# Sums of weight blocks tied to the heads of the attention, and feed-forward operands in six steps instead of five

## The chip, the cores and the metric

The kernel runs on one core of one Trainium2 chip. The core has five engines that run side by side, each through an instruction list of its own, in order: TensorE (PE, matrix products), VectorE (DVE), ScalarE (ACT), GpSimd (POOL) and SyncE (SP), which issues transfers. POOL and ACT issue transfers as well. The metric is the time of one execution on the device in microseconds (us), less is better.

## The reference

The reference is one decoder block in float32 over a sequence of 1024 tokens of width 1024. Two branches read one normalised input, are merged by gates and pass one output projection. Then follow a cross-attention into 256 memory tokens, a feed-forward part and a last norm.

```python
u = rms_norm(h, norm_mix[l])
proj = u @ w_in[l]
u_ssm, q, k, v, f_logit, gate_logits = jnp.split(proj, [...], axis=-1)
y_ssm = jax.nn.gelu(s5_ssm(u_ssm, ...))              # 32 groups, 64 states each
glu_a, glu_b = jnp.split(y_ssm @ w_glu[l], 2, axis=-1)
out_a = glu_a * jax.nn.sigmoid(glu_b)
att = forgetting_attention(q, k, v, f_logit + b_forget[l])   # 8 heads of 64, causal
out_b = att @ w_fox_o[l]
gate_a, gate_b = jnp.split(jax.nn.sigmoid(gate_logits), 2, axis=-1)
h = h + (gate_a * out_a + gate_b * out_b) @ w_mix_out[l]
h = h + memory_cross_attention(...)                  # 4 heads of 128
f_a, f_b = jnp.split(rms_norm(h, norm_ffn[l]) @ w_ffn_in[l], 2, axis=-1)
h = h + (jax.nn.silu(f_a) * f_b) @ w_ffn_out[l]
return rms_norm(h, norm_final)
```

## The kernel before

**Numbers.** Each float32 operand of a matrix product is split into a rounded part "hi" and a remainder "lo" (split, L182 to 184: ACT casts, DVE subtracts), and a product is three matmuls, hi by hi, hi by lo and lo by hi (mm3, L171 to 175). PE's work of one such product over 128 rows, 128 columns and 512 tokens is therefore three instructions.

**Stages in the order of time.** The entry stage norms the input and the memory tokens, projects keys, values and the state-space branch's input u, and stores u to DRAM (u_d, L516, issued by SP). The state-space stage (stage_ssm, L534) runs 32 gate steps of 24 matmuls each on PE, and between them, by a table of positions, four quarters of the state-space branch. A quarter's weights are made by S5.weights (L1504 to 1557): POOL makes the tables fre and fim (L1522 to 1525) and EC and ES (L1546 to 1556). PE transposes fre and fim (turn_weights, L1568), with a MEMSET of a buffer Ts on POOL in the same step (L1577). ACT copies Ts to Tt (L1586), and the quarter's result is computed from Tt by L1651 and L1652. The inputs xg of a quarter are read back from u_d (L1593).

The attention (Fox.run, L1947) follows, head by head. A head has 12 units, a unit being 128 keys by up to 512 queries: scores on PE (L1872), an exponential pf on ACT (L1888), its rounded part ph, and its remainder pl = pf - ph. In four of the 12 units POOL subtracts (L1891), in eight DVE does (L1894). PE multiplies the values by ph and later by pl (values_hi, values_lo at L1913). When a head is complete, finish (L1919) brings the row sums to SP's queue three times: rc (L1924), rd_d (L1926) and a broadcast rb (L1928), whose instruction is kept in self.spread[h]. max_row (L1860) stores the next head's row maxima, hb<-mr (L1869), also on SP; the next head's first scores read them. Work for later heads (projections, loads of weight blocks raw at L1789 and L1790) is put into "side lists", one for each unit, and traced behind that unit's scores. Heads 5 to 7 also load the state-space result y and the gated tiles' weights.

The tail (stage_tail, L600) starts with eight gated tiles (L719 to 729): a value product, copied by DVE to sg (L1327), a gate product whose sigmoid sb ACT computes, and their product (L1333). Beside them, ahead(0) (L663 to 716) prepares the operands of the feed-forward part's first tile. They are fetched (fetch), split (plain), summed in block form (sums), and split once more (seventh, the tile wph, and rest), and each result is stored by ACT into w_d. It is a list of five functions, of which one is called in each of the tiles 0, 2, 3, 4 and 5. For the second tile, the same list is woven between the products of the memory queries (L843 and 844).

**The mixer's weight sums.** The output projection w_mix_out is multiplied in a block scheme with seven products instead of eight. Four of these need sums of the weight's 512 x 512 blocks, kept in a DRAM tile mt_d under the numbers 4 to 7. mix_sums (L583 to 597) makes them by transfers alone, in six steps. SP copies two blocks of 1 MB to sums 5 and 7 (L594). POOL adds a second block to each by accumulating transfers from DRAM to DRAM (L592), two of 0.5 MB for each sum. SP copies sum 5 to sum 6 (L596), and POOL adds to it; SP copies sum 6 to sum 4 (L597), and POOL adds to that. In all there are four copies and eight accumulating transfers. They are needed when the mixer's product loads them (L743), behind the gated tiles.

**What sets the order.** The kernel is traced once, and a scheduler then arranges each engine's list by its own model of times and by the data that instructions need, so that an instruction can stand far ahead of the place where it was traced. `B.behind(ins)` (L146) limits this: instructions that are traced inside the block and run on the engine of `ins` stay behind `ins`. It says nothing on other engines. The six steps are traced one for each of the heads 1 to 6, in the side list of unit 1, without such a limit:

```python
            if h == 0:
                side[0].append(lambda: self.values_of_v(0, 7))
            elif h < 7:
                side[1].append(sums[h - 1])
```

Of the kernel before, what the change touches and what calls it, by code (L numbers as in the profile page):

```python
# [14 lines left out]
ALU = mybir.AluOpType  # L15
# [51 lines left out]
def f32(ap):  # L67
    return ap.bitcast(F32)
# [37 lines left out]
class Shared:  # L106
# [5 lines left out]
    def tmp(self, name, dt=F32):  # L112
        return self.pool.tile([P, D], dt, tag="tmp", bufs=5, name=name)
# [469 lines left out]
def mix_sums(B, w, mt_d):  # L583


    S, G = B.S, B.G
    blk = w.rearrange("(p two k) (c n) -> two c k p n", two=2, k=P, c=2)
    dst = {n: mt_d[n].rearrange("p k n -> k p n") for n in (4, 5, 6, 7)}

    def add(n, i, j):  # L590
        for p in (0, 2):
            G.dma_start(dst[n][:, p:p + 2], blk[i, j, :, p:p + 2], accum_op=ALU.add)  # L592

    return [lambda: (S.dma_start(dst[5], blk[0, 0]), S.dma_start(dst[7], blk[0, 1])),  # L594
            lambda: (add(5, 0, 1), add(7, 1, 1)),
            lambda: S.dma_start(dst[6], dst[5]), lambda: add(6, 1, 1),  # L596
            lambda: S.dma_start(dst[4], dst[6]), lambda: add(4, 1, 0)]  # L597


def stage_tail(B, big, s2, sh, x, glu, aT, gate_d, kv_d, mt_d, w_fox_o, w_mix_out, g_mq, w_mem_q, w_mem_o, g_ffn,  # L600
               w_ffn_in, w_ffn_out, g_fin, out):
    nc, V, A, G, T, S, small, ident = B.nc, B.V, B.A, B.G, B.T, B.S, B.small, B.ident
# [5 lines left out]
    def slot(dt=F32, name="t"):  # L608
        return s2.tile([P, D], dt, tag="t", bufs=NS2, name=name)
# [12 lines left out]
    def fox_part(j):  # L622
        if j % 2 == 0:
            with B.behind(glu.after):
                fox[j // 2] = B.wblock(w_fox_o, 0, 4, j * P, 2 * P)
        fh, fl = fox[j // 2]
        o = (j % 2) * P
        sg = glu.out.pop(j)
        for h in range(2):
            cs = slice(512 * h, 512 * h + 512)  # L630
            po = B.bank(("pv", "pv", "misc")[(2 * j + h) % 3])
            B.gemm_t(po, fh[:, :, o:o + P], fl[:, :, o:o + P], aT, h, 4)
            gb = load(gate_d[D + j * P:D + (j + 1) * P, cs], "gb")
            V.tensor_mul(gb, gb, po)
            n = ((None, 1), (4, 2))[j % 2][h]
            dst = block(n, j // 2) if n else sg[:, cs]
            V.tensor_add(dst, sg[:, cs], gb)
        if j % 2 == 0:
            gs[j // 2] = sg[:, :512]
            V.tensor_sub(block(7, j // 2), block(1, j // 2), gs[j // 2])  # L640
        else:
            merged_pair(j // 2)
# [16 lines left out]
    AHEAD_IN = 2  # L659
    w_d = B.dram.tile([AHEAD_IN + 1, 7, P, D], F32, name="w_d")  # L660
    pre = {}

    def ahead(j, tmp=tmp):  # L663

        def keep(n, t_):
            A.dma_start(w_d[j, n], f32(t_))

        def pair(n):
            hl = tmp("wph", F32R), tmp("wpl", F32R)
            return hl, [[t_[:, o:o + 512] for t_ in hl] for o in (0, 512)]  # L670

        def fetch():
            pre[j] = [tmp("wpr") for _ in range(2)]
            for r_, c in zip(pre[j], (0, FH)):
                S.dma_start(r_.rearrange("p (k c) -> p k c", k=8),
                            w_ffn_in[:, c + j * P:c + (j + 1) * P].rearrange("(k p) c -> p k c", p=P))

        def plain():
            hl, _ = pair(0)
            B.split(*hl, pre[j][0])  # L680
            for i, t_ in enumerate(hl):
                keep(i, t_)

        def sums():
            ra, rb = pre[j]
            b22 = rb[:, 512:]
            hl, (w5, w6) = pair(2)
            V.tensor_add(ra[:, 512:], ra[:, 512:], b22)
            V.tensor_add(ra[:, :512], ra[:, :512], rb[:, :512])
            V.tensor_add(rb[:, :512], rb[:, :512], b22)  # L690
            B.split(*w5, ra[:, :512])
            V.tensor_add(ra[:, 512:], ra[:, 512:], ra[:, :512])
            V.tensor_add(ra[:, :512], ra[:, :512], b22)
            B.split(*w6, ra[:, :512])
            for i, t_ in enumerate(hl):
                keep(2 + i, t_)

        def seventh():
            e_ = tmp("wph", F32R)
            B.split(e_[:, :512], e_[:, 512:], pre[j][1][:, :512])  # L700
            keep(4, e_)

        def rest():
            ra, rb = pre.pop(j)
            hl, (w3, w4) = pair(5)
            B.split(*w3, rb[:, 512:])
            B.split(*w4, ra[:, 512:])
            for i, t_ in enumerate(hl):
                keep(5 + i, t_)

        def first():
            pre[j] = [tmp("wpr")]
            S.dma_start(pre[j][0].rearrange("p (k c) -> p k c", k=8),
                        w_ffn_in[:, j * P:(j + 1) * P].rearrange("(k p) c -> p k c", p=P))

        return [fetch, plain, sums, seventh, rest] if j < AHEAD_IN else [first, plain]

    first = ahead(0, lambda name, dt=F32: slot(dt, name))
    for j in range(8):  # L719
        if j > 3:  # L720
            with B.behind(glu.after):
                for f in glu.values(j):
                    f()
        glu.rest(j)
        if j in (0, 2, 3, 4, 5):
            first.pop(0)()
        if j > 2:
            fox_part(j - 3)
# [86 lines left out]
    def norm(t, gb, act, banks=("misc", "pv")):  # L815
        xs = s2.tile([P, D], F32, tag="xs", bufs=1, name="xs")
        B.norm_scale(xs, H[t], B.rstd(H[t]), gb)
        return B.norm_turn(xs, act, t, banks)
# [17 lines left out]
    def mem_q(h, hf):  # L836
        ps = B.bank()
        B.gemm_t(ps, *wq[h], u2, hf, 8)
        B.split(*qT.rhs(h, hf), ps)

    normed = []
    turns = [lambda t=t: normed.append(norm(t, gq, u2)) for t in range(4, 8)]
    weave([lambda h=h: mem_q(h, 0) for h in range(MH)],  # L843
          [f for i in range(4) for f in turns[i:i + 1] + later[3 * i // 2:3 * (i + 1) // 2]])
    kth, ktl, vh, vl = [slot(F32R, "kv") for _ in range(4)]
    gf = B.bcast_gain(s2, g_ffn)
    sc = float(DH * 2) ** -0.5
# [303 lines left out]
    for j in range(2, NF):  # L1151
# [9 lines left out]
        f = w_fetch(j + 2) if j + 2 < NF else f  # L1161
# [504 lines left out]
class Fox:  # L1666
# [280 lines left out]
    def run(self, y_d, yT, aT, w_glu, w_d, filler, sums):  # L1947
        B, fp, S = self.B, self.fp, self.B.S
# [14 lines left out]
        def first_glu(i, f):  # L1963
            with B.behind(self.spread[3] if i < 9 else self.maxima[NH - 2]):
                f()
# [36 lines left out]
        for h in range(NH):  # L2002
            side = {i: [] for i in range(12)}
            late = h == NH - 2
            if late:
                for i, f in enumerate(pro[h + 1].parts[8:]):
                    side[i // 2].append(f)
                side[3].append(pro[h + 1].evac[1])
            if h + 1 < NH:
                for i, f in enumerate(self.row_max(h + 1)):  # L2010
                    side[(RSLOT_LATE if late else RSLOT)[i]].append(f)
                side[9].append(lambda: self.max_row(h + 1))
            if h + 2 < NH:
                n = 8 if h + 3 == NH else 16
                for i, f in enumerate(pro[h + 2].parts[:n]):
                    side[i if n == 8 else PSLOT[i]].append(f)
                side[9].append(pro[h + 2].evac[0])
                if n == 16:
                    side[11].append(pro[h + 2].evac[1])
            if h + 3 < NH:  # L2020
                side[9].append(lambda: pro[h + 3].split(self.exp))
            for n_ in {1: (4, 5), 2: (6,), 3: (7,)}.get(h, ()):
                side[5].append(lambda n_=n_: pro[n_].load(self.spread[h - 1]))
            if h == 0:
                side[0].append(lambda: self.values_of_v(0, 7))
            elif h < 7:
                side[1].append(sums[h - 1])
            if late:
                for k in range(8):
                    side[4 + k].append(lambda k=k: load_y(k % 4, k // 4))  # L2030
            if h == NH - 1:
                for k in range(3):
                    side[6 + k].append(lambda k=k: load_att(k))
                for i, f in enumerate(filler):
                    side[i * 12 // len(filler)].append(lambda i=i, f=f: first_glu(i, f))
            for i, u in enumerate(units):
                self.scores(h, *u)
                for f in side[i]:
                    f()
                if len(self.hi_todo) > 2:  # L2040
                    self.values_hi()
                if len(self.lo_todo) > 1:
                    self.values_lo()
                if h and i == 5:
                    with B.behind(self.left):
                        self.divide(h - 1)
# [34 lines left out]
```

## Time and profile before

| | |
|---|---|
| three runs | 1579.6, 1583.47 and 1584.05 us |
| median of them | 1583.47 us |
| the profiled execution | 1580.27 us |
| its span, first to last instruction | 1578.0 us |
| mean granted clock of PE in it | 0.984 of full speed |

By stages, from the view that gives the busy time of each engine in a stretch of the span:

| stretch, us | about what runs | PE busy | DVE busy | POOL busy | granted clock | DMA share |
|---|---|---|---|---|---|---|
| 0 to 160 | entry, first quarter of the state space | 123.49 | 75.25 | 42.18 | 0.88 | 0.74 |
| 160 to 400 | state space, first head's projections | 234.09 | 124.00 | 80.44 | 0.99 | 0.50 |
| 400 to 640 | attention | 237.22 | 182.97 | 44.99 | 1.00 | 0.40 |
| 640 to 800 | end of attention, gated tiles, mixer | 156.21 | 138.08 | 21.24 | 0.99 | 0.64 |
| 800 to 1000 | mixer, memory attention | 198.47 | 141.29 | 26.36 | 1.00 | 0.34 |
| 1000 to 1578 | feed-forward, last norm | 570.38 | 377.46 | 44.67 | 1.00 | 0.56 |

The profile is one execution, recorded by the hardware. Busy time is the time in which an engine has an instruction under way. Issuing a transfer is not counted as busy. The granted clock is the share of TensorE's full speed that the chip allowed it. DMA share is the mean busy share of the core's 16 DMA engines. A line such as "POOL L592" names the engine and the line of the kernel; "out<-in" names the tiles. A row of the waits gives, for a line, its total idle time ahead, the number of waits and the longest, with the instruction that ended them behind "<-".

### The profile page before, as it was taken

Reading aid. Unit: us, or ns where it says so; the run is one execution under the profiler, and the core shown is the slowest. Engines: PE = TensorE matmul, PEld = TensorE weight load, DVE = VectorE, ACT = ScalarE, POOL = GpSimd, SP = SyncE. Lnnn points to the kernel's source line nnn. Section 1 sums busy time; section 2 is a strip of 40 time slices with the busy share of each in tenths; the row PEclk is TensorE's granted clock in tenths of the full one; section 3 lists DMA queues with packets and bytes.
Section 4 is the critical chain, followed back from the end, with each engine's and each line's share of the span. In section 5 each row is a group of like instructions: output and inputs, shape, how many; then the busy total and the mean of one; then the engine's idle time right before and its main releaser. Section 6 shows DMA issues by size and latency. Waiting matters only on the chain.

```text
span 1578.0 us, 20402 instructions
## 1 busy us (share of the span) xinstructions
PE 1519.8 (96%) x7281; PEld 1255.2 (80%) x7281; DVE 1039.0 (66%) x1860; ACT 669.5 (42%) x1187; POOL 259.9 (16%) x349
## 2 busy tenths in 40 slices
PE   8983899999999999999999999999999999999998
PEld 7873788889877768788888888888888888888886
DVE  7910755334678876868975687777666777565555
ACT  6411233332466764223545564333333333354343
POOL 1115654210012112310001200010000000101001
PEclk9995999999999999999999999999999999999999
DMA  9865455761123374847702156455555443896652
GB/s 281 200 120 153 81 141 122 144 192 26 11 49 64 96 191 134 265 152 253 240 30 67 41 193 220 154 161 160 162 162 164 154 147 124 286 392 225 199 161 107
DMA packets 201061, 245.59 MB, mean 156 GB/s; under 512 B 35736, under 2 KB 127816, under 8 KB 200448
## 3 DMA queue, kind: packets, MB, share of 16 engines
q1 hardware_dynamic: 191296, 222.27, 47.5%
q10 hardware_dynamic: 7488, 17.83, 2.9%
q0 software_dynamic: 2176, 4.19, 1.7%
q8 instruction: 57, 0.93, 0.2%
q14 instruction: 44, 0.36, 0.1%
HBM read 173.47 MB, written 81.10 MB: 161 GB/s over the span
## 4 chain that ended last, share of the span: by engine, by line
PE 79%; DVE 7%; issue 5%; DMA 4%; POOL 2%; ACT 2%; SPq 0%; ACTq 0%; POOLq 0%; DVEq 0%
PE mm L1053 15%; PE pv L1053 8%; PE mm L173 6%; PE mm L175 6%; PE mm L174 6%; PE mm L1196 5%; PE sc L1053 4%; PE sc L1196 4%; PE pv L1196 3%; PE sc L173 2%; PE sc L175 2%; PE sc L174 2%; PE mm L761 2%; PE misc L1196 2%; DMA mt_d<-in_w_mix_out_dram 1%
## 5 line engine op out<-in xcount | busy, mean ns | idle before, releaser
L183 ACT CAST whi<-raw 128x1024 fp32r<-128x1024 f32 (+2 forms) x122 | 111.0, 913 | 105.3 <-PE mm L174 36.2
L184 DVE TENSOR_TENSOR wlo<-raw,whi 128x1024 fp32r<-128x1024 f32 (+2 forms) x122 | 128.7, 1060 | 39.1 <-ACT whi L183 36.4
L184 DVE TENSOR_TENSOR ol<-or,oh 128x1024 fp32r<-128x1024 f32 x73 | 90.0, 1235 | 73.3 <-ACT oh L183 72.3
L173 PE MATMUL mm<-uh,whi 128*128 128x512 f32 x344 | 137.7, 400 | 0.0
L174 PE MATMUL mm<-ul,whi 128*128 128x512 f32 x344 | 136.1, 396 | 0.0
L175 PE MATMUL mm<-uh,wlo 128*128 128x512 f32 x344 | 135.4, 394 | 0.0
L183 ACT CAST oh<-or 128x1024 fp32r<-128x1024 f32 x73 | 76.9, 1056 | 104.8 <-PE mm L1196 34.1
L1086 POOL TENSOR_TENSOR g<-a,c 128x512 f32<-128x512 f32 x22 | 35.7, 1621 | 387.8 <-ACT a L1085 387.8
L175 PEld LDWEIGHTS mm<-uh,wlo 128*128 128x128 f32 x344 | 65.3, 190 | 13.7 <-DVE wlo L184 0.2
L1891 POOL TENSOR_TENSOR pl<-pf,ph 128x512 fp32r<-128x512 f32 (+1 forms) x32 | 37.8, 1182 | 230.3 <-DVE ph L1890 191.1
L173 PEld LDWEIGHTS mm<-uh,whi 128*128 128x128 f32 x344 | 65.5, 190 | 11.8
L174 PEld LDWEIGHTS mm<-ul,whi 128*128 128x128 f32 x344 | 65.5, 190 | 11.2
L1075 DVE SCALAR_TENSOR_TENSOR c<-c,pv 128x512 f32<-128x512 f32 x22 | 15.1, 688 | 78.6 <-ACT c L1074 78.5
L1888 ACT ACTIVATE pf<-sc 128x512 f32<-128x512 f32 (+1 forms) x96 | 46.6, 490 | 44.2 <-DVE sc L1884 28.4
L211 POOL TENSOR_TENSOR r<-ms,mhalf 128x1 f32<-128x1 f32 (+1 forms) x26 | 16.3, 631 | 295.3 <-DVE ms L207 253.7
L1053 PE MATMUL pv<-S3h,we 128*128 128x512 f32 x176 | 57.8, 389 | 0.0
L1539 DVE TENSOR_TENSOR Gm<-w,w 64x512 f32<-64x512 f32 x8 | 5.5, 683 | 66.4 <-POOL w L1534 66.4
L173 PE MATMUL mm<-yh,whi 128*128 128x512 f32 x104 | 41.5, 399 | 3.8 <-DVE sg L1327 3.8
L1894 DVE TENSOR_TENSOR pl<-pf,ph 128x512 fp32r<-128x512 f32 (+2 forms) x64 | 35.3, 553 | 10.3 <-ACT ph L1893 9.6
L1196 PE MATMUL mm<-ol,oh 128*128 128x512 f32 (+1 forms) x110 | 41.9, 381 | 0.0
L1196 PE MATMUL mm<-oh,ol 128*128 128x512 f32 (+1 forms) x110 | 41.9, 381 | 0.0
L1196 PE MATMUL mm<-oh 128*128 128x512 f32 (+1 forms) x110 | 41.9, 381 | 0.0
(661 smaller groups left out, 4627.1 us busy)
## 6 DMA issues: line engine op xcount, KB each, us to landing
or<-c_d SPq DMA_DIRECT2D x77, 256.0 KB
wo<-in_w_ffn_out_dram SPq DMA_DIRECT2D x22, 512.0 KB
c_d<-g SPq DMA_DIRECT2D x44, 256.0 KB
t_d<-wo SPq DMA_DIRECT2D x44, 256.0 KB
or<-t_d SPq DMA_DIRECT2D x44, 256.0 KB
rawb<-in_w_ffn_in_dram SPq DMA_DIRECT2D x20, 512.0 KB
raw<-in_w_ffn_in_dram SPq DMA_DIRECT2D x20, 512.0 KB
raw<-in_w_in_dram SPq DMA_DIRECT2D x19, 512.0 KB
```

Source lines behind the costliest of these rows:

```text
L173: T.matmul(ps, lh, rh, start=first, stop=False)
L174: T.matmul(ps, lh, rl, start=False, stop=False)
L175: return T.matmul(ps, ll, rh, start=False, stop=last)
L183: cast = self.A.copy(hi, src)
L184: self.rest = (self.G if pool_lo else self.V).tensor_sub(lo, src, f32(hi))
L761: T.matmul(ps, l_[:, gi], r_[:, c:c + 512], start=k == 0 and p == 0 and n in (1, 2, 7), stop=p == 3 and k == 2, skip_group_check=True)
L1053: T.matmul(ps, l_[:, k, :], r_, start=first and k == 0 and i == 0, stop=k == 3 and i == 2, skip_group_check=True)
L1086: G.tensor_mul(g[:, 512:], a1, c1)
L1196: T.matmul(ps, l_[:, gi], r_[:, c0:c1], start=k == 0 and (p == NP - LAST if own else p == 0 and n in (1, 2, 7)), stop=p == NP - 1 and k == ...
L1888: self.exp = A.activation(pf[:, off:], ps[:, off:], AF.Exp)
L1891: G.tensor_sub(pl[:, off:], pf[:, off:], f32(ph[:, off:]))
L1894: self.left = V.tensor_sub(pl[:, off:], pf[:, off:], f32(ph[:, off:]))
```

## The change

The six steps of mix_sums take an instruction `after`, and each step's transfers are traced inside `B.behind(after)`. Step h is now traced in the side list of unit 5 of head h, and `after` is the broadcast rb of the head before (self.spread[h - 1]), an instruction of SP. In the tail, `sums` is cut in two, `sums` and `more`, so that ahead(0) and ahead(1) are lists of six functions. ahead(0)'s run in the tiles 1 to 6, and the weave with the memory queries takes its seven functions by 7 * i // 4 instead of 3 * i // 2. No instruction is added or removed; line numbers grow by 6 behind mix_sums and by 11 behind ahead.

```diff
--- before.py
+++ after.py
@@ -583,18 +583,24 @@
 def mix_sums(B, w, mt_d):
 
 
-    S, G = B.S, B.G
     blk = w.rearrange("(p two k) (c n) -> two c k p n", two=2, k=P, c=2)
     dst = {n: mt_d[n].rearrange("p k n -> k p n") for n in (4, 5, 6, 7)}
 
+    def put(n, src):
+        B.S.dma_start(dst[n], src)
+
     def add(n, i, j):
         for p in (0, 2):
-            G.dma_start(dst[n][:, p:p + 2], blk[i, j, :, p:p + 2], accum_op=ALU.add)
-
-    return [lambda: (S.dma_start(dst[5], blk[0, 0]), S.dma_start(dst[7], blk[0, 1])),
-            lambda: (add(5, 0, 1), add(7, 1, 1)),
-            lambda: S.dma_start(dst[6], dst[5]), lambda: add(6, 1, 1),
-            lambda: S.dma_start(dst[4], dst[6]), lambda: add(4, 1, 0)]
+            B.G.dma_start(dst[n][:, p:p + 2], blk[i, j, :, p:p + 2], accum_op=ALU.add)
+
+    steps = [lambda: (put(5, blk[0, 0]), put(7, blk[0, 1])), lambda: (add(5, 0, 1), add(7, 1, 1)),
+             lambda: put(6, dst[5]), lambda: add(6, 1, 1), lambda: put(4, dst[6]), lambda: add(4, 1, 0)]
+
+    def step(f, after):
+        with B.behind(after):
+            f()
+
+    return [lambda after, f=f: step(f, after) for f in steps]
...
@@ -682,13 +688,18 @@
...
         def sums():
-            ra, rb = pre[j]
+            ra, rb = pre[j][:2]
             b22 = rb[:, 512:]
             hl, (w5, w6) = pair(2)
...
             B.split(*w5, ra[:, :512])
+            pre[j] += [hl, w6]
+
+        def more():
+            ra, rb, hl, w6 = pre[j]
+            b22 = rb[:, 512:]
             V.tensor_add(ra[:, 512:], ra[:, 512:], ra[:, :512])
             V.tensor_add(ra[:, :512], ra[:, :512], b22)
             B.split(*w6, ra[:, :512])
...
-        return [fetch, plain, sums, seventh, rest] if j < AHEAD_IN else [first, plain]
+        return [fetch, plain, sums, more, seventh, rest] if j < AHEAD_IN else [first, plain]
...
-        if j in (0, 2, 3, 4, 5):
+        if 0 < j < 7:
             first.pop(0)()
...
-          [f for i in range(4) for f in turns[i:i + 1] + later[3 * i // 2:3 * (i + 1) // 2]])
+          [f for i in range(4) for f in turns[i:i + 1] + later[7 * i // 4:7 * (i + 1) // 4]])
...
             elif h < 7:
-                side[1].append(sums[h - 1])
+                side[5].append(lambda: sums[h - 1](self.spread[h - 1]))
```

The first place is POOL in the entry stage, ahead of the first quarter's weights (ld and bb are tables of the state space, xt a tile of tokens that is normed). Before:

```order
L211 TENSOR_TENSOR r_653<-ms_652,mhalf 128x2
L229 TENSOR_TENSOR xt<-xt,gain 128x1024 x2
L592 DMA mt_d<-in_w_mix_out_dram 128x2x512 x8
L1522 TENSOR_TENSOR w_1107<-ld_re,bb_re 128x448
L1523 TENSOR_TENSOR w_1108<-ld_im,bb_im 128x448
```

After:

```order
L211 TENSOR_TENSOR r_653<-ms_652,mhalf 128x2
L229 TENSOR_TENSOR xt<-xt,gain 128x1024 x2
L1533 TENSOR_TENSOR w_1107<-ld_re,bb_re 128x448
L1534 TENSOR_TENSOR w_1108<-ld_im,bb_im 128x448
L1536 COPY fre<-bb_re 128x4x16
```

The eight accumulating transfers are no longer there; the first weight instruction follows the tiles of the norm. On SP, the four copies of mt_d have likewise gone from between the loads of the entry stage and the stores of u_d.

The second place is SP in the attention, in head 1 (behind the broadcast rb that closes head 0 and a first pair of loads; raw are weight blocks of a later head, att_d takes the divided output of head 0, hb is what head 2's scores read, mr are its row maxima). Before:

```order
L1789 DMA raw<-in_w_in_dram 128x8x64
L1790 DMA raw<-in_w_in_dram 128x8x64
L1940 DMA att_d<-ahi 64x1024
L1940 DMA att_d<-alo 64x1024
L1829 DMA hb_3272<-cum_d 2x1024
L1869 DMA hb<-mr 1x8x128
```

After:

```order
L1800 DMA raw<-in_w_in_dram 128x8x64
L1801 DMA raw<-in_w_in_dram 128x8x64
L590 DMA mt_d<-in_w_mix_out_dram 128x4x512 x2
L1951 DMA att_d<-ahi 64x1024
L1951 DMA att_d<-alo 64x1024
L1880 DMA hb<-mr 1x8x128
L1840 DMA hb_3272<-cum_d 2x1024
```

The two copies of step 1 stand behind the loads raw and ahead of the stores of att_d and of hb<-mr.

The third place is POOL in the attention; the numbers of the tiles tell the units apart. In each head, the row of 256 elements is the first of POOL's four subtractions. Before (the end of head 1, and heads 2 and 3):

```order
L1891 TENSOR_TENSOR pl_4191<-pf_4192,ph_4190 128x512
L1891 TENSOR_TENSOR pl_4334<-pf_4335,ph_4333 128x256
L1891 TENSOR_TENSOR pl_4386<-pf_4387,ph_4385 128x512
L1891 TENSOR_TENSOR pl_4439<-pf_4440,ph_4438 128x512
L1891 TENSOR_TENSOR pl_4481<-pf_4482,ph_4480 128x512
L1891 TENSOR_TENSOR pl_4621<-pf_4622,ph_4620 128x256
L1891 TENSOR_TENSOR pl_4673<-pf_4674,ph_4672 128x512
L1891 TENSOR_TENSOR pl_4726<-pf_4727,ph_4725 128x512
L1891 TENSOR_TENSOR pl_4768<-pf_4769,ph_4767 128x512
```

After:

```order
L1902 TENSOR_TENSOR pl_4191<-pf_4192,ph_4190 128x512
L594 DMA mt_d_2967<-in_w_mix_out_dram 128x2x512 x4
L1902 TENSOR_TENSOR pl_4330<-pf_4331,ph_4329 128x256
L1902 TENSOR_TENSOR pl_4382<-pf_4383,ph_4381 128x512
L1902 TENSOR_TENSOR pl_4439<-pf_4440,ph_4438 128x512
L1902 TENSOR_TENSOR pl_4481<-pf_4482,ph_4480 128x512
L1902 TENSOR_TENSOR pl_4620<-pf_4621,ph_4619 128x256
L1902 TENSOR_TENSOR pl_4672<-pf_4673,ph_4671 128x512
L1902 TENSOR_TENSOR pl_4726<-pf_4727,ph_4725 128x512
L594 DMA mt_d_2967<-in_w_mix_out_dram 128x2x512
L1902 TENSOR_TENSOR pl_4768<-pf_4769,ph_4767 128x512
L594 DMA mt_d_2967<-in_w_mix_out_dram 128x2x512
```

The four additions of step 2 stand between head 1's last subtraction and head 2's first, one of step 4 ahead of head 3's last subtraction and one behind it. Those of step 6 stand together ahead of the last subtraction of head 5. On PE, 12 matmuls of a projection now stand ahead of head 2's first scores.

More of the change, by code (lines that the diff above doesn't have):

```diff
@@ L703, in rest @@
         def rest():
-            ra, rb = pre.pop(j)
+            ra, rb = pre.pop(j)[:2]
             hl, (w3, w4) = pair(5)
```

## The prediction

> **What bounds the kernel now.** I read the page's head first, for the engine that fills the span.
>
> ```profile
> span 1578.0 us, 20402 instructions
> PE 1519.8 (96%) x7281; PEld 1255.2 (80%) x7281; DVE 1039.0 (66%) x1860; ACT 669.5 (42%) x1187; POOL 259.9 (16%) x349
> PE   8983899999999999999999999999999999999998
> PEclk9995999999999999999999999999999999999999
> ```
>
> TensorE (PE) is the bound. It is visibly idle in one place, the fourth slice (118 to 158 us), and there its clock is halved too. So a change that moves transfers can gain where PE waits, and only there. The waits of PE, longest first, say where:
>
> ```profile
> PE pv L1568 <- POOL ES L1547: 26.5, 1, 26.5
> PE pv L1651 <- ACT Tt L1586: 5.9, 1, 5.9
> PE pv L1568 <- POOL fim L1524: 3.8, 1, 3.8
> PE mm L173 <- DVE sg L1327: 3.8, 1, 3.8
> ```
>
> The first three are the state-space stage's first quarter (its weights are made on GpSimd, POOL). The fourth is the gated tiles. Busy time by stretch, for the clock (columns: stretch, length, busy PE, PEld, DVE, ACT, POOL, granted clock, DMA share, GB/s):
>
> ```profile
> 113.40:140.00 26.60, 0.10 (x2) 0.04 (x1) 0.00 (x0) 2.75 (x4) 5.78 (x10) 0.57 0.85 207
> 140.00:160.00 20.00, 16.16 (x68) 13.91 (x69) 4.58 (x6) 3.52 (x8) 18.75 (x43) 0.63 0.23 65
> 160.00:200.00 40.00, 34.09 (x154) 28.73 (x154) 28.65 (x41) 12.34 (x20) 24.90 (x50) 0.91 0.44 81
> 200.00:240.00 40.00, 40.00 (x214) 34.42 (x213) 20.77 (x29) 15.40 (x26) 22.86 (x46) 1.00 0.54 138
> ```
>
> The second quarter (200:240) has no wait and the full clock, so the three waits are no property of the stage's arithmetic. What POOL did instead, by the timeline:
>
> ```profile
> 74.72 1.36 POOL L592 DMA_DIRECT2D mt_d<-in_w_mix_out_dram  x1 [25.75 <-DMA mt_d<-in_w_mix_out_dram]
> 81.28 1.17 POOL L592 DMA_DIRECT2D mt_d<-in_w_mix_out_dram  x1 [5.20 <-issue]
> 87.78 1.15 POOL L592 DMA_DIRECT2D mt_d<-in_w_mix_out_dram  x1 [5.34 <-issue]
> 98.37 1.16 POOL L592 DMA_DIRECT2D mt_d<-in_w_mix_out_dram  x1 [9.44 <-issue]
> 104.90 1.15 POOL L592 DMA_DIRECT2D mt_d<-in_w_mix_out_dram  x1 [5.37 <-issue]
> 110.77 1.15 POOL L592 DMA_DIRECT2D mt_d<-in_w_mix_out_dram  x1 [4.72 <-issue]
> 123.59 1.15 POOL L592 DMA_DIRECT2D mt_d<-in_w_mix_out_dram  x1 [11.67 <-DMA mt_d<-mt_d]
> 135.37 1.15 POOL L592 DMA_DIRECT2D mt_d<-in_w_mix_out_dram  x1 [10.63 <-issue]
> 136.09 1.44 POOL L1522 TENSOR_TENSOR w<-ld_re,bb_re 128x448 f32<-128x448 f32 x1
> ```
>
> Eight accumulating transfers stand ahead of the first weight instruction, and each is held for 4.7 to 10.6 us before it issues, though it takes only 1.15 us itself. An instruction that is no transfer follows after 0.72 us (135.37 to 136.09). So one accumulating transfer is cheap for POOL, and a row of them blocks it. The operands that POOL needs were there at 81.1 us:
>
> ```profile
> 80.70 0.43 DVE L1479 TENSOR_TENSOR bb_im<-bb_im,tb 128x256 f32<-128x256 f32 x1
> ```
>
> **Part 1, what goes: the eight transfers ahead of the weights.** In the new order nothing of mt_d stands on POOL or SP there. PE's idle time is 26.5 + 3.8 + 5.9 = 36.2 us. The clock adds 16.16 x (1 - 0.63) = 6.0 and 34.09 x (1 - 0.91) = 3.1, in all 45 us. What is late next? POOL's way from L1522 to the end of fim took 136.1 to about 145, 9 us, so it could end near 90. But a MEMSET that stands ahead of fim's last instruction waits until the u_d stores have landed. SP's queue held those, too, behind the copies of mt_d:
>
> ```profile
> 116.98 0.55 SPq L597 DMA_DIRECT2D mt_d<-mt_d  x1
> 120.02 1.55 SPq L516 DMA_DIRECT2D u_d<-us  x2
> 132.10 0.60 ACT L554 ACTIVATE gs<-sc 128x512 f32<-128x512 f32 x1 [28.89 <-DMA u_d<-us]
> ```
>
> Their last source is written at 93 us, so I put the landing near 102 (the last store landed some 10 us after its issue, 121 to 132), and fim near 105. PE asks at 113.4: 8 us of cover. Tt and St have five gate steps of 5.4 us (24 matmuls at 0.227 us) between, enough in the later quarters. I keep 2 us for a remainder (bounds 0 and 6): **-43 us**.
>
> **Part 2, the same transfers in the attention.** The SP puts of 1 MB are tied behind a head's last broadcast; POOL's additions have no tie of their own (it binds instructions of SP, the engine of the broadcast) and follow by their data. The order puts four additions between head 1's last subtraction on POOL and head 2's first:
>
> ```profile
> 459.93 1.29 POOL L1891 TENSOR_TENSOR pl<-pf,ph 128x512 fp32r<-128x512 f32 x1 [4.08 <-DVE ph L1890]
> 472.39 0.75 POOL L1891 TENSOR_TENSOR pl<-pf,ph 128x256 fp32r<-128x256 f32 x1 [11.16 <-DVE rc L1925]
> 476.49 0.28 PE L1913 MATMUL pv<-pl,vhi 128*65 128x256 f32 x1
> ```
>
> The hole there is 11.2 us, and PE reads that pl at 476.5, 3.4 us after it is ready. Now the puts: SP gets to them behind these loads.
>
> ```profile
> 454.94 2.04 SPq L1790 DMA_DIRECT2D raw<-in_w_in_dram  x1
> 457.08 2.52 SPq L1940 DMA_DIRECT2D att_d<-ahi  x1
> 464.05 0.70 SPq L1869 DMA_DIRECT2D hb<-mr  x1
> ```
>
> The queues are 0.59 busy there (the stretches, last column but one):
>
> ```profile
> 455.00:460.00 5.00, 5.00 (x23) 3.47 (x22) 4.87 (x11) 3.95 (x7) 0.93 (x2) 1.00 0.59 88
> 460.00:465.00 5.00, 5.00 (x26) 3.66 (x25) 4.45 (x11) 4.15 (x8) 1.23 (x1) 1.00 0.59 161
> ```
>
> And a 1 MB copy, from issue to landing on a queue that was empty, by the chain of waits:
>
> ```profile
> 116.98 6.21 DMA mt_d<-mt_d
> ```
>
> Issued at 457, the first put lands at 463.2 at best; behind the traffic that lasts to 465, at 471 at worst; I take 468. Four additions need three intervals, 18.6 us (three of 6.2, from 98.37, 104.90, 110.77) to 23.65 (74.72 to 98.37), and 0.7 for the last. So POOL is free at about 489.5, the subtraction ends at 490.3, and everything on PE after 476.5 is 14 to 15 us late (bounds 483.3 and 496.1, or 7 and 20 us). hb<-mr, which head 2's first scores need at 467.6, stands behind 2 MB on the same queue; the order has put 12 projection matmuls (2.7 us) ahead of those scores, and what PE loses there lies inside the 14 to 15. After a wait PE runs at half clock: after the 5.9 us wait from 186.98 to 192.4, after the 3.8 us one from 670.7 to 673.7. Two such phases of 3 to 5.4 us cost half their length, 3 to 5 us. **+19 us** (8 to 25).
>
> [...]
>
> The third step (1 MB copy) and its two additions fall into head 3, the fifth and its two into head 5. By the same 6.2 us each, the first addition of a pair stands ahead of the head's last subtraction in head 3, and both of them in head 5:
>
> ```profile
> 552.83 1.28 POOL L1891 TENSOR_TENSOR pl<-pf,ph 128x512 fp32r<-128x512 f32 x1 [2.09 <-DVE ph L1890]
> 558.09 1.30 POOL L1891 TENSOR_TENSOR pl<-pf,ph 128x512 fp32r<-128x512 f32 x1 [3.98 <-DVE ph L1890]
> ```
>
> In head 5: first at 554, second at 562, subtraction at 563 and not 558.1, less some 3 us of cover: 2 to 3 us. In head 3 about the same, and the loads of y behind the last copy start 4 us later. **+6 us** (0 to 14).
>
> **Part 3, the feed-forward operands in six steps.** The split leaves VectorE's order nearly as it was: both halves of the sums still stand between the same sg instructions. One thing moves: the fifth operand's subtraction (wph, 0.68 us), with its cast and store on ScalarE.
>
> ```profile
> 659.20 0.68 DVE L184 TENSOR_TENSOR wph<-wpr,wph 128x512 fp32r<-128x512 f32 x1
> 660.92 1.21 DVE L1333 TENSOR_TENSOR sg<-sg,sb 128x512 f32<-128x512 f32 x1 [1.04 <-ACT sb L1332]
> 669.62 1.06 DVE L1327 COPY sg<-mm 128x512 f32<-128x512 f32 x1
> ```
>
> The store made ScalarE late with sb, hence the 1.04 us. Both go from the run-up to the copy that PE waits for: 1.7 of 3.8 us, and 1.5 us of half clock: **-3 us** (0 to -5). The fetch that starts one tile later, and the same split for the second tile in the weave with the memory queries, hide beside a PE that is full there: 0.
>
> **Sum.** -43 + 19 + 6 - 3 = -21. The profiled execution took 1580.27 us; it is near the low end of the three runs (1579.6, 1583.47, 1584.05). 1580.27 - 21 = 1559.3; I add about 1 us toward the median: **1560 us**.
>
> **The rivals.**
> - **The additions cost little** (0.2): the put lands at 463 and the intervals are 6.2 us, so PE is 7 us late in head 2 with 2 us of clock, and 2 us elsewhere: -43 - 3 + 11 = -35, 1545 us. For it: the uncontended intervals at 98 to 111. Against: 9.4 and 10.6 us of holding wherever other traffic ran. [...]
> - **Dearer attention, or a remainder in the first quarter** (0.2): part 2 at its 25, head 3 and 5 at 10, or Tt late by 6: -10 to -14, about 1568 us.
> - **Nothing gained** (0.04): the additions stay ahead on POOL because no tie binds them. The new order speaks against it. Part 3 alone: about 1577, within 0.3% of before.
> - **Slower** (0.04): each addition is held 11.8 us (123.59 to 135.37), since the attention loads the queues throughout. Then head 2 waits 468 + 36 + 0.7 + 0.8 - 476.5 = 29 us, head 3 and 5 some 9 each, and the half clock and the y loads 6 more: 53 against 46, about 1587 us. It decides where the attention's loss passes 46 us, which needs additions of about 11 us.
>
> **How the numbers follow.** Forecast 0.52, then 0.2, 0.2, 0.04, 0.04. Its own range is 1551 to 1566; the cheap case reaches down to 1540, the dear one up to 1574; I give **1540 to 1574**. About 0.3% (4.7 us) is what a measurement of this kernel can tell from no change. Faster 0.92, same 0.04, slower 0.04.
>
> **What would show it.** Right: no wait of PE on POOL between 113 and 200 us and full clock in every slice there; the fim instruction before 113 us; in head 2 one PE wait of 9 us or more on a POOL subtraction, after four accumulating transfers spaced over 6 us. Wrong: a PE wait on Tt or on a DMA near 145 us; head 2 without a wait; a wait over 25 us; the wait at the gated tiles as long as before.

## The result

| | before | after |
|---|---|---|
| median, us | 1582.6 (1579.6 to 1584.05, 4 runs) | 1571.22 (1570.13 to 1573.65, 4 runs) |
| ratio after to before | | 0.9933, 95% interval 0.9913 to 0.9952 |
| profiled execution / its span, us | 1580.27 / 1578.0 | 1571.02 / 1569.0 |

The change takes 11.4 us off, 0.7%: the way that was forecast, inside the range of 1540 to 1574, and about half of the 21 us of the forecast's sum. One execution of the run e1 below was slow as a whole (2160.76 us, at a granted clock of 0.654) and is left out of its median. The head of the page of after (share of the span, busy tenths in 40 slices, granted clock in tenths):

```profile
span 1569.0 us, 20397 instructions
PE   8999999999967989999999999999999999999998
PEclk9999999999978999999999999999999999999999
```

The dip of the fourth slice is gone, and new ones stand in the slices from 431 to 510 us, with the clock, and from 549 us. Two rows of the waits of PE after (line, what ended the wait, total us, times, longest) matter here, the longest and the one on the row maxima:

```profile
PE pv L1924 <- POOL pl L1902: 29.3, 3, 14.4
PE sc L1892 <- DMA hb<-mr: 0.5, 1, 0.5
```

The three waits of the state-space stage and the one on sg have left the list, and three waits on POOL's subtractions are new: 14.4, 10.1 and 4.8 us, in heads 2, 3 and 5. But for some matmuls that change places inside the heads, PE runs the same ones in the same order in both kernels, so the start of the n-th can be compared where it is the same instruction. The lead of after over before, worked out that way:

| at the n-th matmul, place | start before, us | start after, us | lead, us |
|---|---|---|---|
| 540, entry stage | 112.2 | 112.2 | 0 |
| 780, end of the first quarter | 203.2 | 158.3 | 44.8 |
| 2100, attention, head 1 | 435.0 | 390.2 | 44.8 |
| 2400, end of head 2 | 496.3 | 472.6 | 23.7 |
| 2580, head 4 | 533.6 | 522.3 | 11.3 |
| 2880, head 6 | 598.1 | 594.4 | 3.7 |
| 3240, gated tiles | 683.8 | 674.8 | 9.0 |
| 7200, near the end | 1554.4 | 1545.5 | 9.0 |

So 44.8 us were won, 41.1 were lost again in heads 2, 3 and 5 (21.1, 12.4 and 7.6), and 5.3 won at the gated tiles. POOL's timeline after shows the losses:

```profile
83.59 1.15 POOL L1535 TENSOR_TENSOR fre<-w,w 128x448 f32<-128x448 f32 x1
96.69 1.16 POOL L1535 TENSOR_TENSOR fim<-w,w 128x448 f32<-128x448 f32 x1
...
424.44 1.36 POOL L594 DMA_DIRECT2D mt_d<-in_w_mix_out_dram  x1 [7.91 <-DMA mt_d<-in_w_mix_out_dram]
431.36 1.19 POOL L594 DMA_DIRECT2D mt_d<-in_w_mix_out_dram  x1 [5.57 <-issue]
438.10 1.15 POOL L594 DMA_DIRECT2D mt_d<-in_w_mix_out_dram  x1 [5.55 <-DMA rb<-rd_d]
448.05 1.16 POOL L594 DMA_DIRECT2D mt_d<-in_w_mix_out_dram  x1 [8.80 <-issue]
448.77 1.19 POOL L1902 TENSOR_TENSOR pl<-pf,ph 128x256 fp32r<-128x256 f32 x1
...
497.68 1.16 POOL L594 DMA_DIRECT2D mt_d<-in_w_mix_out_dram  x1 [15.91 <-DMA mt_d<-mt_d]
498.44 1.70 POOL L1902 TENSOR_TENSOR pl<-pf,ph 128x512 fp32r<-128x512 f32 x1
...
543.22 1.16 POOL L594 DMA_DIRECT2D mt_d<-in_w_mix_out_dram  x1 [0.41 <-DMA mt_d<-mt_d]
551.00 1.15 POOL L594 DMA_DIRECT2D mt_d<-in_w_mix_out_dram  x1 [6.62 <-issue]
551.72 1.72 POOL L1902 TENSOR_TENSOR pl<-pf,ph 128x512 fp32r<-128x512 f32 x1
```

Fre and fim are done at 85 and 98 us, ahead of PE's demand at 113.4. Each of the three waits of PE ends with a subtraction that stands behind an addition. In head 3 POOL stands idle for 15.91 us in front of the first addition, which waits for the copy of sum 5 to sum 6. SP's queue says when that copy was issued and behind what:

```profile
475.31 0.58 SPq L1800 DMA_DIRECT2D raw<-in_w_in_dram  x1
475.94 0.57 SPq L1801 DMA_DIRECT2D raw<-in_w_in_dram  x1
476.63 6.44 SPq L590 DMA_DIRECT2D mt_d<-mt_d  x1
```

From the copy's issue to the addition's are 21 us; the forecast had used 6.2. What remained open was why, and whether the loss is POOL's list or the transfers' traffic.

### The profile page after: what moved, and what is told of

It is laid out like the page before. It is cut to its first block, busy times and chain, and to the rows that moved or that the text cites. A ratio compares the mean times of both kernels' runs of the same rounds, so it can differ in the third digit from the quotient of the medians.

```text
span 1569.0 us, 20397 instructions
## 1 busy us (share of the span) xinstructions
PE 1521.0 (97%) x7281; PEld 1255.0 (80%) x7281; DVE 1039.4 (66%) x1860; ACT 668.2 (43%) x1187; POOL 268.6 (17%) x349
## 4 chain that ended last, share of the span: by engine, by line
PE 87%; DVE 4%; DMA 3%; issue 2%; ACT 2%; POOL 1%; SPq 0%; POOLq 0%; DVEq 0%; ACTq 0%
PE mm L1064 15%; PE pv L1064 8%; PE mm L174 7%; PE mm L173 7%; PE mm L175 7%; PE mm L1207 5%; PE sc L1064 4%; PE sc L1207 4%; PE sc L173 3%; PE sc L175 3%; PE sc L174 3%; PE pv L1207 3%; PE mm L772 2%; DMA mt_d<-mt_d 2%; PE misc L1207 2%
## 5 line engine op out<-in xcount | busy, mean ns | idle before, releaser
L174 PEld LDWEIGHTS mm<-ul,whi 128*128 128x128 f32 x344 | 65.9, 192 | 11.3
L1924 PE MATMUL pv<-pl,vhi 128*65 128x512 f32 (+1 forms) x96 | 33.8, 356 | 29.7 <-POOL pl L1902 29.3
L1924 PEld LDWEIGHTS pv<-pl,vhi 128*65 128x65 f32 x96 | 13.5, 142 | 35.6 <-POOL pl L1902 30.6
L1351 POOL TENSOR_TENSOR sg<-sg,ga 128x512 f32<-128x512 f32 x16 | 29.3, 1852 | 74.0 <-DMA ga<-gate_d 38.6
```

What stands on the lines that cost most here:

```text
L174: T.matmul(ps, lh, rl, start=False, stop=False)
L1924: self.B.T.matmul(ps[0:65, off:], self.vh[kt // 2][:, kt % 2, h, :], pl[:, off:], start=False, stop=last)
```

## The experiments

Each loss given below is the lead lost between the same matmuls as above (2100 to 2400 is head 2, to 2580 head 3, to 2880 heads 4 to 6).

**1. Five feed-forward steps again (e1).** The edit puts `sums` back together and the list back to five:

```diff
-        return [fetch, plain, sums, more, seventh, rest] if j < AHEAD_IN else [first, plain]
+        return [fetch, plain, sums, seventh, rest] if j < AHEAD_IN else [first, plain]
-        if 0 < j < 7:
+        if j in (0, 2, 3, 4, 5):
```

> The changed kernel with the feed-forward operands in five steps again, as before; the tied transfers stay. Theory (the split itself takes the wait at the gated tiles away): the wait of PE on the copy to sg comes back with about 3.8 us, with 1.5 us of half clock behind it, so about 1571.2 + 5.3 = 1576.5 us. Rival (the wait went because transfers or loads of the attention moved, not by the split): 1571 to 1572 us and no wait on sg.

Measured: 1575.24 us, ratio to before 0.9969 (0.9955 to 0.9984). The time is near the theory's and the reason is not: the wait on sg is not back.

```profile
PE mm L173 <- DVE sg L1333: 0.6, 1, 0.6
```

The gated tiles still gain 4.5 us on before, against 5.3 with six steps. Of the other 4.3 us between the two profiled executions, 2.7 arise in the attention (losses 22.0, 12.9 and 8.9) and 1.1 ahead of it, where the edit does not change any engine's order. So most of the wait went without the split: the copy that PE waited for starts at 666.59 us here and at 669.62 before, while PE is at the same matmul within 0.2 us. Followed back along VectorE's list, the 3 us begin with the row sums of the last head. SP issues their broadcast rb when the store rd_d of 4 KB has landed. First before, then e1:

```profile
618.04 0.32 SPq L1926 DMA_DIRECT2D rd_d<-rc  x1
621.52 0.47 SPq L1928 DMA_DIRECT2D rb<-rd_d  x1
```

```profile
618.26 0.32 SPq L1932 DMA_DIRECT2D rd_d<-rc  x1
619.66 0.47 SPq L1934 DMA_DIRECT2D rb<-rd_d  x1
```

In before, VectorE waits 1.70 us for rb at 625.62 us and in e1 not at all. SP issues the loads wpr, which stand behind the stores of VectorE's result, 2.7 us later (633.89 against 631.21), and ScalarE's cast of wpr is 3.1 us later. The packets of the two traces tell the store apart: of its 128 pieces of 32 bytes, eight move in before only as another packet ends, at 620.4 us, one of 16384 bytes on the queue that the views call "instruction". In e1 all pieces are through by 619.27 us, ahead of such a packet.

**2. The copy ahead of the loads (e2).**

```diff
-                side[5].append(lambda n_=n_: pro[n_].load(self.spread[h - 1]))
+                side[5].append(lambda n_=n_: pro[n_].load(sums[2](self.spread[2]) if n_ == 7 else self.spread[h - 1]))
```

> The changed kernel with one thing turned round in head 3: the copy of sum 5 to sum 6 is issued on SP ahead of the two loads raw, and these behind it. Theory (the copy was late because it stood behind two loads in pieces of 256 bytes on one queue, and the additions inherit that): the copy lands within about 8 us of its issue, the first addition of head 3 issues 7 to 9 us after it and not 21, PE's wait of 10.3 us in head 3 is gone or under 2 us, and the time is about 1571.2 - 12 = 1559 us. Rival (a copy inside DRAM is slow in the attention, whatever stands ahead): the wait stays within 2 us of 10.3 and the time at 1569 to 1572 us.

Measured: 1575.44 us, ratio 0.9973 (0.9958 to 0.9988): no gain, the theory missed. POOL's timeline:

```profile
484.18 1.27 POOL L594 DMA_DIRECT2D mt_d<-in_w_mix_out_dram  x1 [2.85 <-DMA mt_d<-mt_d]
500.35 1.15 POOL L594 DMA_DIRECT2D mt_d<-in_w_mix_out_dram  x1 [14.90 <-issue]
501.06 1.73 POOL L1902 TENSOR_TENSOR pl<-pf,ph 128x512 fp32r<-128x512 f32 x1
```

The copy, issued at 474.92, was done in 9.3 us, close to what was expected. But now the first addition ran beside the loads and held POOL for 14.9 us. And the scheduler put the second addition ahead of the last subtraction too, so this run is no clean test of the order on the queue; e9 and e10 try it again.

**3. A `dynamic_dma_scratch_size` of 3584 instead of 1024 (e3).**

```diff
-    nc = _bacc.Bacc("TRN2", target_bir_lowering=False, num_devices=1, dynamic_dma_scratch_size=1024)
+    nc = _bacc.Bacc("TRN2", target_bir_lowering=False, num_devices=1, dynamic_dma_scratch_size=3584)
-        gs = qp.tile([P, 512], F32, tag="gs", bufs=3, name="gs")
+        gs = qp.tile([P, 512], F32, tag="gs", bufs=2, name="gs")
```

> The changed kernel with 3584 instead of 1024 bytes of room for the descriptors that POOL writes, and two instead of three buffers for the gate results (to find the space). Theory A (POOL is held because the room takes only one transfer): three transfers can be on their way, the four additions of head 2 issue within 3 to 10 us instead of 24, PE's waits in heads 2 and 5 go, the one in head 3 stays since there POOL waits for the copy's data: about 1571.2 - 27 = 1544 us. Theory B (accumulating transfers are issued one after the other whatever the room): issues stay 6 us and more apart, 1570 to 1575 us.

Measured: 1561.73 us, ratio 0.9887 (0.9864 to 0.991). The issues of the additions are as theory A has them:

```profile
426.62 4.88 POOL L594 DMA_DIRECT2D mt_d<-in_w_mix_out_dram  x4 [5.37 <-DMA mt_d<-in_w_mix_out_dram]
434.62 0.73 POOL L1902 TENSOR_TENSOR pl<-pf,ph 128x256 fp32r<-128x256 f32 x1 [3.12 <-DVE ph L1901]
```

Four additions issue in 4.9 us instead of 24. But head 2, head 3 and heads 4 to 6 still lose 8.6, 11.0 and 7.7 us (and some 3 us go ahead of them; which of the two edits costs them was not tried), where A had only head 3 left. Waits on other names took the places of heads 2 and 5:

```profile
PE pv L1924 <- POOL pl L1902: 8.9, 1, 8.9
PE mm L1862 <- DVE mc L1867: 4.3, 2, 3.1
PE sc L1892 <- DMA hb<-mr: 3.8, 1, 3.8
```

**4. All six steps where POOL is idle (e4).** The puts of step 1 follow the state-space stage's last shift, the additions of step 2 POOL's last product there, and the rest the copies of the gated tiles' weights (SP) and the last mask (POOL), ahead of head 0:

```diff
+        for i, f in enumerate(sums):
+            f((shifted, turned, last, self.tied)[min(i, 2 + i % 2)])
...
-            elif h < 7:
-                side[5].append(lambda: sums[h - 1](self.spread[h - 1]))
```

> The changed kernel with all six steps taken out of the heads and put where POOL has nothing to do between the state-space stage and head 0 (from about 275 to 346 us). Theory (what the attention lost is POOL's list being held by the additions, not the transfers as such): no wait of PE on POOL in the attention, full clock there; of 1571.2 us go the 41 us that the heads lost: about 1530 us, with up to 6 us more if a store of cum_d or a load of hb ahead of head 0 is held behind the copies. Rival (the same transfers cost PE the like wherever they run, by their traffic): 1555 us or more.

Measured: 1533.53 us, ratio 0.9709 (0.9686 to 0.9732). The theory's time, and the attention loses 0.2 us in all. POOL's timeline:

```profile
278.60 1.37 POOL L594 DMA_DIRECT2D mt_d<-in_w_mix_out_dram  x1
286.36 1.17 POOL L594 DMA_DIRECT2D mt_d<-in_w_mix_out_dram  x1 [6.39 <-issue]
303.43 1.15 POOL L594 DMA_DIRECT2D mt_d<-in_w_mix_out_dram  x1 [15.89 <-issue]
...
368.03 1.15 POOL L594 DMA_DIRECT2D mt_d<-in_w_mix_out_dram  x1 [11.07 <-issue]
376.01 0.74 POOL L1902 TENSOR_TENSOR pl<-pf,ph 128x256 fp32r<-128x256 f32 x1 [6.83 <-DVE ph L1901]
```

Additions are held up to 15.9 us here, longer than the 8.8 us in the heads, and cost nothing, since nothing that PE needs soon stands behind them. The traffic costs PE nothing here either. This version beats both kernels.

**5. POOL's subtractions in VectorE's list (e6), and the additions left out (e7).** Two cuts through the attention's loss: e6 keeps all transfers and takes the subtractions from behind them (all four of head 2, the last of heads 3 and 5); e7 leaves the additions out, so that its sums are incomplete.

```diff
-            G.tensor_sub(pl[:, off:], pf[:, off:], f32(ph[:, off:]))
+            (V if h == 2 or (h in (3, 5) and (qc, kt) == (1, 4)) else G).tensor_sub(pl[:, off:], pf[:, off:], f32(ph[:, off:]))
```

```diff
         for p in (0, 2):
-            B.G.dma_start(dst[n][:, p:p + 2], blk[i, j, :, p:p + 2], accum_op=ALU.add)
+            pass
```

> The changed kernel with POOL's four subtractions of head 2 and its last ones of heads 3 and 5 given to VectorE; all transfers stay where they are. Theory (PE loses because its subtractions stand in POOL's list behind the additions): the three waits of 14.6, 10.3 and 5.0 us go, with their half clock; left are waits of under 4 us for small transfers on SP and up to 3 us of VectorE's extra work: 1571.2 - 41 + 5 = 1535 us. Rival (the transfers' traffic alone delays hb, rb and the loads as much): waits on other names take their place, 1555 us or more.

> The changed kernel without the eight accumulating transfers (the sums are then wrong); the four copies on SP stay. Theory (the additions cost the attention, the copies next to nothing): 1571.2 - 41 + 1 = 1531 us, no wait of PE on POOL. Rival (the copies of 1 MB ahead of att_d and hb on SP's queue carry a good part of the loss): 1540 us or more, with waits on hb or a projection's operands.

Measured: 1552.67 us (ratio 0.9833, 0.9802 to 0.9863) and 1540.88 us (0.9755, 0.9729 to 0.9781). Neither theory holds in full: e6 lies between theory and rival, nearer to the rival's 1555 us, and e7 meets its rival's 1540 us. No wait of PE on POOL is left in either, and another wait comes up in its place. First e6, then e7:

```profile
PE sc L1892 <- DMA hb<-mr: 6.5, 3, 4.4
```

```profile
PE sc L1891 <- DMA hb<-mr: 5.1, 2, 4.4
```

The copies alone cost the attention 11.1 us (4.1, 6.4 and 0.6; e7), most of it with the small transfer of the row maxima, which SP sends behind a copy: 5.1 us of waits, and about 2.2 us of half clock behind the longer one. Copies and additions with no subtraction behind them cost 18.2 (e6, VectorE's extra work included, in a profiled execution 4 us under the median). The full 41 needs the subtractions behind the additions.

**6. The loads in larger pieces (e8).** One load of 128 columns in pieces of 512 bytes replaces the two loads of head 3. It takes other columns, so the last head gets other weights:

```diff
+                if h == 7:
+                    return S.dma_start(rv, self.w_in[:, C_Q:C_Q + 128].rearrange("(k p) c -> p k c", p=P))
```

> The changed kernel with the two loads raw of head 3 (of the last head's weights, 64 columns in pieces of 256 bytes each) as one load of the same 128 columns' worth in pieces of 512 bytes (other columns, so the last head is wrong). Theory (these loads, at some 100 pieces a microsecond, hold the DMA engines, so that the copy behind them, or the addition beside them, is late): the load's pieces are gone in 6 us or less after their start, not 17; the first addition of head 3 issues within 13 us of the copy and not 21; PE's wait in head 3 falls from 10.3 to under 4 us: about 1562 us. Rival (the loads have no part in it): wait 9 to 12 us and 1569 to 1573 us.

Measured: 1566.17 us, ratio 0.9917 (0.9887 to 0.9947), halfway: the first addition of head 3 issues 10.7 us after the copy (476.71 to 487.41), PE's wait there is 5.3 us instead of 10.1, and head 3 loses 7.5 us instead of 12.4. Here too both additions stand ahead of the last subtraction: the second issues at 493.54 us and the subtraction starts at 494.25, so that with the changed kernel's order, in which the subtraction stands ahead of the second addition, PE would hardly have waited; that was not run.

**7. Pairs behind the last subtraction (e9), and with the copy first (e10).** The tie now names an instruction of POOL too, and e10 has e2's edit as well:

```diff
-                side[5].append(lambda: sums[h - 1](self.spread[h - 1]))
+                side[5].append(lambda: sums[h - 1](self.spread[h - 1], self.pooled[h - 1]))
```

> The changed kernel with each pair of additions of steps 4 and 6 tied behind POOL's last subtraction of heads 3 and 5 too (the tie of the change binds SP alone); SP's order is as it was. Theory (these pairs cost PE because they stand ahead of a subtraction; what is behind them then is the next head's first subtraction, 10 us later): the wait of 10.3 us in head 3 goes, the copy still lands some 20 us after its issue, the pair issues at about 497 and 504, and the first subtraction of head 4, which PE wants near 500, is 4 to 7 us late; head 5 loses nothing to POOL; a wait of about 4.5 us on hb appears in head 3. Sum 1571.2 - 12 - 7.6 + 6 + 5 = 1562 us. Rival (the place in POOL's list does not matter, the transfers' traffic does): 1568 us or more.

> The same, and the copy of head 3 ahead of the two loads raw on SP. Theory (with the copy ahead of the loads the pair is done earlier): the copy lands within 9 us of its issue, the first addition issues at about 486, the second, held by the loads' pieces, at about 500, head 4's first subtraction is at most 2 us late; the wait on hb in head 3 stays: about 1562 - 4 = 1558 us. Rival (copy and additions beside the loads take as long in either order): the same time as with the loads ahead, within 2 us.

Measured: 1565.94 us (ratio 0.9904, 0.9886 to 0.9921) and 1566.03 us (0.9903, 0.9885 to 0.9921). They are 5.3 us under the changed kernel, in ratios to before whose intervals overlap (the changed kernel's is 0.9913 to 0.9952), so the reading rests on the waits. The place in POOL's list matters: of the three waits on POOL only head 2's is left. The waits of e9:

```profile
PE pv L1925 <- POOL pl L1903: 15.1, 1, 15.1
PE pv L1918 <- DVE ph L1902: 4.8, 1, 4.8
PE sc L1893 <- DMA hb<-mr: 4.5, 1, 4.5
```

Head 3 loses 9.1 us instead of 12.4, now to the row maxima; heads 4 to 6 lose 6.4 us instead of 7.6, to a stall of VectorE on the row sums, which travel beside the additions and the loads of y:

```profile
558.20 0.20 DVE L1937 RECIPROCAL rc<-rc 128x8 f32<-128x8 f32 x1 [4.18 <-DMA rc<-num]
```

That second wait was not expected. E10's time is the same as e9's, as its rival has it. But since the row maxima end PE's wait in head 3 there too (5.4 us), the run can't say how copy and additions alone compare.

**8. Five steps against six, with the attention undisturbed (e5 and e4; e12 and e11 on one chip).**

E5 and e12 are e4 with e1's edit, and e11 is e4 once more.

> The kernel with the steps in POOL's idle stretch (1533.5 us), with the feed-forward operands in five steps again. Theory (the split takes the wait on sg away, which in the run with five steps was hidden only because the attention was late and the loads of the gated tiles early): the wait on sg is 3.8 us instead of 1.4, with its half clock 1.5 to 4 us more, about 1536 us. Rival (the split has no part in it): wait 1.4 us and 1532 to 1535 us.

> The kernel with the steps in POOL's idle stretch and six feed-forward steps, once more, on one chip with the next: 1533.5 us, wait on sg 1.4 us.

> The same with five steps, on the same chip: wait on sg 3.8 us; theory (the split is worth what it takes from that wait and its half clock): 3 to 5 us more than with six. Rival (the split is worth nothing): within 1.5 us.

Measured: five steps 1537.66 (e5; ratio 0.9738, 0.9712 to 0.9764) and 1536.99 us (e12; 0.9725, 0.9707 to 0.9744), six steps 1533.53 (e4) and 1533.37 us (e11; 0.9696, 0.9678 to 0.9714): 4.1 and 3.6 us apart, the same way twice (e11 and e12 on one chip, where every execution of the one is under every one of the other). The waits on sg of e5, e12, e4 and e11:

```profile
PE mm L173 <- DVE sg L1333: 3.8, 1, 3.8
```

```profile
PE mm L173 <- DVE sg L1333: 4.0, 1, 4.0
```

```profile
PE mm L173 <- DVE sg L1338: 1.4, 1, 1.4
```

```profile
PE mm L173 <- DVE sg L1338: 2.3, 1, 2.3
```

So the split does what it was forecast to do where the attention runs as it did before. In all four, as in before, rb follows rd_d by 3.1 to 3.5 us; in the changed kernel and the other eight runs it follows by 1.4 us. Why the packet of the instruction queue comes ahead of the store's last pieces in the former and behind them in the latter was not tried.

## Why the prediction came out as it did

| step | forecast, us | by the traces, us |
|---|---|---|
| part 1, state-space stage | -43 (waits 36.2, clock 9, remainder 2) | -44.8 |
| part 2, head 2 | +19 (8 to 25) | +21.1 |
| part 2, heads 3 and 5 | +6 (0 to 14) | +20.0 (12.4 and 7.6) |
| part 3, gated tiles | -3 (0 to -5) | -5.3 |
| sum | -21 | -9.0 |

**Part 1 was right**, without the remainder of 2 us: PE is full from 97 to 160 us, at full clock. This is most of the stretch in which it had waited before (columns: stretch, length, busy PE, PEld, DVE, ACT, POOL, granted clock, DMA share, GB/s):

```profile
113.00:140.00 27.00, 27.00 (x141) 23.03 (x140) 20.09 (x29) 8.01 (x17) 15.62 (x16) 1.00 0.45 75
```

The MEMSET behind the u_d stores held POOL until 95.9 us and not 105.

**Part 2, head 2, was right** in time and mechanism. The first addition issued at 424.4 (468 forecast, less the lead of 44.8: 423), the four took 24.3 us to the next subtraction (21.5 forecast), and PE waited 14.4 us (14 to 15). The two phases of half clock are there too, 450 to 453.5 us behind the wait and this one ahead of it, together some 4.7 us (3 to 5 forecast):

```profile
429.60:435.60 6.00, 5.94 (x20) 4.65 (x19) 3.43 (x14) 2.11 (x6) 1.19 (x1) 0.50 0.51 67
```

What the holding of the additions one by one hangs on, which the forecast took from rows without a reason, e3 shows: with a `dynamic_dma_scratch_size` of 3584 instead of 1024 (and one buffer fewer for the gate results) the four issue in 4.9 us instead of 24.

**The step that failed is the last one of part 2: "In head 5: first at 554, second at 562, subtraction at 563 and not 558.1, less some 3 us of cover: 2 to 3 us. In head 3 about the same".** In head 5 the instants were right: with the lead of 11.3 us added, the rows stand at 554.5, 562.3 and 563.0. But there was no cover. The 3 us are those of heads 2 and 3 (3.4 and 2.7 us in before); in head 5 of before the subtraction ends at 559.39 us and PE's matmul that waits for it starts 0.4 us later:

```profile
559.83 0.40 PE L1913 MATMUL pv<-pl,vhi 128*65 128x512 f32 x1
```

So PE waited 4.8 us, and then ran at half clock, a term that the forecast counted for head 2 alone:

```profile
553.50:559.30 5.80, 5.80 (x18) 4.83 (x19) 1.27 (x6) 0.85 (x3) 0.00 (x0) 0.50 1.14 264
```

The two waits, 10.1 and 4.8 us, with half of the 4.5 and 5.8 us at half clock behind them, make up the 20.0 us.

In head 3 the mechanism was the same and its size was not: the copy's 6.2 us came from a row on an empty queue, and here it took 21 us beside two loads in pieces of 256 bytes. The trace of before held the warning: the same loads, in the same place, slow down there. A line of the transfers' view for 501 to 508 us of before:

```profile
DMA packets 739, 0.20 MB, mean 28 GB/s; under 512 B 736, under 2 KB 736, under 8 KB 739
```

E8 shows these loads' part in it: with one load of other columns, in larger pieces, 10.7 us. E2 shows that the order on the queue is not the whole of it, since an addition beside the loads is held as well.

**What lies beneath the waits on POOL** was left out of the sum, and e6, e7 and e9 show it: the row maxima and row sums, stored in transfers of 4 KB, are late behind and beside the copies (PE waits 6.5, 5.1 and 4.5 us for hb<-mr in e6, e7 and e9, and VectorE 4.18 us for rc<-num in e9). In the changed kernel this is mostly hidden in the waits on POOL (0.5 us on hb<-mr), and it would be next. Whether such a transfer waits out the copies ahead of it on SP's queue was not shown: e7's longer wait, 4.4 us, is not isolated from the traffic of other queues.

**Part 3** came out larger than forecast, by luck. In the changed kernel the split gave 0.8 us at the gated tiles (5.3 against 4.5 in e1). The other 4.5 us came with the last head's row sums, whose store landed 2.1 us sooner than in before (rb behind rd_d by 1.4 instead of 3.5 us). The forecast had no such term. The forecast's own 1.7 us are shown by e4, e5, e11 and e12, where that store is as late as before: the wait on sg falls by 2.4 and 1.7 us (3.8 to 1.4, 4.0 to 2.3).

**The rivals.** "Dearer attention" came closest (1568 us, chance 0.2), with the extra loss in the heads that it named (head 3 and 5 lost 20 us where it had 10, head 2 21 where it had 25). "The additions cost little" is refuted by the waits. No run with the additions in the heads shows the 1540 us to which the forecast's range lets this case reach: the shortest took 1552.67 us (e6), and an addition of 0.5 MB took at least 5.7 us to land in the changed kernel's trace:

```profile
DMA to landing us min/median/max: 5.7/6.6/9.6
```

## What to carry to other kernels

A transfer that an engine issues belongs to that engine's list: ask what stands behind it there, how long it can be held (up to 8.8 us in the heads of the changed kernel, 15.9 in e4), and tie it by an instruction of the engine that issues it, since a tie on another engine's list leaves the scheduler free to hoist it. Put long rows of such transfers where the issuing engine has nothing to do for PE (1533 us here), not where PE is merely full. Price a transfer from a row beside like traffic, not from a row on an empty queue (21 us against 6.2 here), and add the half clock behind the wait (3.0 to 5.8 us of it in before and after, behind the waits of 3.8, 4.8, 5.9, 10.1 and 14.4 us). And read the cover of each wait from its own row: it was 3.4 us in one head and 0.4 in another.

## What the runs showed that was not expected

The same kind of load, 64 columns in pieces of 256 bytes, runs at very different rates: the transfers' view of before counts 2803 pieces in the 7 us from 452 us (head 1) and 739 in those from 501 us (head 3), where the DMA engines are only 39% busy. First the one, then the other:

```profile
DMA packets 2803, 0.71 MB, mean 102 GB/s; under 512 B 2801, under 2 KB 2801, under 8 KB 2803
```

```profile
q1 hardware_dynamic: 739, 0.20, 39.0%
```

No run tells why; other columns, in larger pieces, were faster (e8). And while they run, an addition that is issued beside them takes 15.9 us to land instead of some 6 (e2), though the engines are not full there either: in the 16 us from 484 us their two queues take 39.0 and 17.8% of them.

Nor was it expected that a wait would go with the landing of a 4 KB store 50 us ahead of it. Whether the packet of the instruction queue comes ahead of its last pieces or behind them goes with the wait on sg in all fourteen traces. Where it comes ahead, the wait is 3.8 to 4.0 us with five steps and 1.4 to 2.3 with six; where it comes behind, at most 0.6.
